# A 64x64 triangular solve in a delta-rule recurrence: blocks of 16 and doubling, or blocks of 32 and substitution

## The chip, the core and the metric

The kernel runs on one core of a Trainium2 chip. The core has five instruction streams that run beside each other and wait for one another through semaphores: the tensor engine (PE, with its weight loads as PEld), VectorE (DVE), ScalarE (ACT), GpSimd (POOL) and SyncE (SP), which here only issues DMAs. Each stream runs its instructions strictly in the order in which they stand. The metric is the device time of one execution in microseconds, as the median of the runs; lower is better.

## What is computed

The reference is a two-layer decoder trunk over 512 tokens of width 1024. Each layer projects its input once and feeds four branches: a delta-rule recurrence (RWKV-7, 8 heads of 64), latent attention, a convolution module and cross-attention. Each branch is gated and projected, the four are merged with sigmoid gates, projected again and normalised. The part that matters here is the recurrence:

```python
def step(state, inp):
    r_t, w_t, k_t, v_t, a_t, b_t = inp
    sa = jnp.einsum('bhvk,bhk->bhv', state, a_t)
    state = (state * w_t[:, :, None, :] + sa[..., None] * b_t[:, :, None, :]
             + v_t[..., None] * k_t[:, :, None, :])
    return state, jnp.einsum('bhvk,bhk->bhv', state, r_t)

s0 = jnp.zeros((B, H, N, N), jnp.float32)
_, y = lax.scan(step, s0, xs)
```

Token by token this would be 512 dependent steps. The kernel takes 64 tokens at a time: inside such a chunk the terms `sa` depend on each other through a strictly triangular 64x64 matrix, so a triangular system has to be solved for each head and chunk; the rest is matrix products.

## The kernel before

**Order.** The kernel is Python that records instructions. A planner (class `Plan`) keeps a clock for each engine and prices each instruction as it is recorded: an instruction on GpSimd, say, at 250 ns and 1.6 ns for each element of a partition, with 105 ns more where it needs the one before it. There is one main stream of tensor work, the items (projections, attention, merges), and beside it many tasks, written as generators. When the planned PE clock reaches the time at which a task can go on, the task's next piece is recorded; otherwise the main stream's next piece is, usually three to fifteen wide matmuls. `plan.due(x)` puts off a task until x is there by the planner's reckoning, and a `yield` of a condition until a counter allows it. A piece that takes PSUM space with "small" is gathered with others, up to 3000 ns, so that PE changes less often between 128x128 tiles and 64x64 ones. What results is one fixed order for each engine and for the SP queue; at run time nothing is reordered, and an engine whose next operand is late waits.

**Units.** The recurrence of a layer is cut into eight units, each of one pair of heads (`j`) and half the tokens (`hf`), so four chunks of two heads, which are eight triangular systems of 64. `rwkv_unit` is the task of one. Several units run overlapped, held apart by counters: `subs` (substitutions done), `mids`, `toks`, `chains`, `units`. The steps of a unit, by the names of their tiles:

- `zw`, `th`, `cum`, `D`, `E`, `bt`, `kt`, `AR`: decay, keys and queries of the unit.
- `g`: the products that give the triangular matrices; VectorE scales and masks them into `M`. A unit could take `g` only when all units before it had finished their substitution (`L["subs"] == un`).
- `Mc`: the diagonal 16x16 blocks of M (four in each system, 32 in a unit), gathered by the block mask `bm`.
- `substitution()`: Mc goes by DMA to a scratch in DRAM (`d1`) and comes back as `W`, one block on each of 32 partitions. GpSimd makes a copy with ones on the diagonal (`zz`, half of `ZT`) and inverts the blocks by 14 steps of two instructions each, then makes a transposed copy. Both go to DRAM (`d2`) and come back as `zc` and `tc`.
- VectorE spreads them into block-diagonal `Z` and `T`. Two rounds of doubling follow on PE: `x0` and `x1` (products with M), `dt`, `dz` and `dy` (products with the inverse so far), each result copied or merged by a mask (`lvm`) on ScalarE or VectorE. After them Z holds the whole inverse of each 64x64 system.
- `nv` (tile `x`, from `NQ` and `vt`) gives half of the right side `RA`; `va` multiplies the inverse by RA.
- `gb`, `hh`, `y0`, `w0` to `w3`, `yb`, `ty`: the chunk's transfer matrices, the chain of states, the outputs and their transposition.

Where other work is: the gate projections `xg`, `mg`, `cg`, `rg`, the merges (`ps_m` and `po`) of branches 3, 1, 2 and 0 in this order, of which the last needs the recurrence's end, and the convolution's taps (`cacc`, on VectorE), its normalisation (`conv_norm`, with the transposes `ct` and `cb`) run in the same time. Weights come in blocks of 512 KB, some blocks ahead of their use, through the same SP queue as the substitution's DMAs.

The tensor engine's products of 64x64 tiles use one quarter of the array each; with `four=True` the planner prices them as running in four quarters at once.

Of the kernel before, what the change touches and what calls it, by code (L numbers as in the profile page):

```python
# [46 lines left out]
for _n, _c in _PARTS:  # L47
# [6 lines left out]
    ("minc", 64), ("bm", 4), ("id2", 64),  # L54
# [207 lines left out]
def trunk_kernel(ctx: ExitStack, tc: tile.TileContext, A, out, dbg=None):  # L262
# [76 lines left out]
    lvm = cp.tile([128, 3, 64], U8, tag="lvm", name="lvm")  # L339
# [3 lines left out]
    scr = [[dp.tile([32 * (n + 1), 256], F32, tag=f"scr{n}{i}", name=f"scr{n}{i}").rearrange("a b -> (a b)") for n in range(2)] for i in range(2)]  # L343
# [13 lines left out]
    def constants():  # L357
        DMA(cst, A["cst"])
        t = u("lvm32", 192, I32)
        DMA(t, A["lvm"])  # L360
        once = u("once", 272)
        DMA(once, A["once"])
        pi = cp.tile([128, 4], I32, tag="pos", name="pos")
        DMA(pi, A["pos"])

        def run():
            V.tensor_copy(lvm, t.rearrange("p (a b) -> p a b", a=3))
# [216 lines left out]
    def layer_items(l):  # L584
# [62 lines left out]
        def begin_rwkv(get):  # L647
# [6 lines left out]
            L["blk"] = [L["rp"].tile([32] + n, F32, tag=x, name=x + t_) for x, n in (("W", [16, 16]), ("ZT", [2, 16, 16]), ("tmpW", [56]))]  # L654
            L["X"] = L["rp"].tile([128, 4, 64], F32, tag="X", name="X" + t_)
            G.memset(L["X"], 0.0)
# [34 lines left out]
        L["units"] = L["chains"] = L["toks"] = L["mids"] = L["subs"] = L["next"] = L["read"] = 0  # L691
# [9 lines left out]
        def rwkv_unit(j, hf, r, k, v):  # L701
# [50 lines left out]
            yield lambda: L["subs"] == un  # L752
# [23 lines left out]
            W, ZT, tmp = L["blk"]  # L776

            zt = []

            def substitution():  # L780
# [8 lines left out]
                plan.due(W)  # L789
                yield  # L790
                zz = ZT[:, 0]
                G.tensor_scalar(out=zz, in0=W, scalar1=1.0, scalar2=0.0, op0=ALU.mult, op1=ALU.add)
                G.memset(zz.rearrange("p a b -> p (a b)")[:, 0:256:17], 1.0)
# [12 lines left out]
                plan.due(d2)  # L806
                yield
                zc, tc_ = rk2("zc", "zc" + t, [4, 16], 2), rk2("tc", "tc" + t, [4, 16], 2)
                dz, dt = (d2[4 * 128 * 16 * i:4 * 128 * 16 * (i + 1)] for i in range(2))
                DMA(tc_, dt.rearrange("(e p t) -> p e t", e=4, t=16))  # L810
                dz = dz.rearrange("(h c p t) -> h p c t", h=2, c=4, t=16)
                for h in range(2):
                    DMA(zc[HALF[h]], dz[h])
                zt.extend((zc, tc_))
                L["subs"] += 1
# [58 lines left out]

            yield lambda: L["subs"] > un
            zc, tc_ = zt
            plan.due(zc, tc_)
            yield
            Z, T, X = rk2("Z", "Z" + t, [4, 64]), rk2("T", "T" + t, [4, 64]), L["X"]
            for dst, src in ((T, tc_), (Z[:, 0:2], chunks(zc)[:, 0]), (Z[:, 2:4], chunks(zc)[:, 1])):  # L880
                n = src.shape[1]
                V.tensor_tensor(out=dst.rearrange("p c (b t) -> p c b t", b=4), in0=src.unsqueeze(2).to_broadcast([128, n, 4, 16]),
                                in1=bm.unsqueeze(1).unsqueeze(3).to_broadcast([128, n, 4, 16]), op=ALU.mult)
            yield

            def second(x, i):

                return x.rearrange("p e (d i k) -> p e d i k", d=2, i=2)[:, :, :, i, :]

            def pairs(x, i):  # L890
                return x.rearrange("p e w -> p (e w)").rearrange("p (e q i k) -> p e q i k", e=2, q=4, i=2)[:, :, :, i, :]

            def four(x):
                return x.rearrange("p e a (d k) -> p e (a d) k", d=2)

            x0, = yield from pg.take([128, 2, 512], "x0" + t, 1, "small")
            xv, nv = (x.rearrange("p c (a w) -> p c a w", a=2) for x in (x0[:, :, 0:64], x0[:, :, 64:192]))
            for cp, c2, h in quads:
                MM(xv[HALF[h], c2, cp].rearrange("p (d k) -> p d k", d=2), M[HALF[c2], 2 * h + cp], second(T, 0)[HALF[c2], 2 * h + cp], start=True, stop=True, four=True)
# [3 lines left out]
            S.copy(pairs(X, 0), four(xv))  # L903
            V.tensor_copy(by2(RA)[:, :, :, 0:64], nv)
            pg.free()
            yield
            x0, = yield from pg.take([128, 2, 512], "dt" + t)
            dT = x0[:, :, 0:64].rearrange("p c (a w) -> p c a w", a=2)
            dz, = yield from pa.take([128, 2, 2, 32], "dz" + t, 1, "small")
            for cp, c2, h in quads:  # L910
                e = 2 * c2 + cp
                MM(dT[HALF[c2], h, cp].rearrange("p (d k) -> p d k", d=2), Z[HALF[h], e], second(X, 0)[HALF[h], e], start=True, stop=True, four=True)
            for cp, c2, h in quads:
                e = 2 * c2 + cp
                MM(dz[HALF[h], c2, cp].rearrange("p (d k) -> p d k", d=2), X[HALF[h], e], second(Z, 1)[HALF[h], e], start=True, stop=True)
            yield

            def lv(i):
                return lvm[:, i, :].rearrange("p (q k) -> p q k", q=4).unsqueeze(1).to_broadcast([128, 2, 4, 16])

            V.copy_predicated(pairs(T, 0), lv(0), four(dT))
# [916 lines left out]
def _constants():  # L1838
    c = {}
# [91 lines left out]
```

## Time and profile before

| what | before |
|---|---|
| median of 3 runs | 1556.57 us (1556.33 to 1556.65) |
| the profiled execution | 1563.89 us |
| its span, first to last instruction | 1562.1 us |
| mean granted clock of PE | 0.994 |
| DMA | 153.34 MB in 81366 packets, 98 GB/s mean |
| recurrence, layer 1: first `g` to last `ty` | 268.5 to about 632 us |
| recurrence, layer 2: the same | 1080.0 to about 1413 us |

The profile is of one execution, which is 7.3 us longer than the median of the runs. Times are microseconds from the start of the span. In a row of instructions the columns are the start, the duration, the engine, the line, the operation and `output<-inputs` with sizes as partitions x elements; numbers of buffers are left out, so tiles of the same name in different units stand under one name. A matmul of 32-bit numbers in these tiles has two records, so eight matmuls show as 16. In a row of windows stand the stretch, its length, the busy time with the number of instructions, the granted clock, the share of DMA and its rate. Lines point to helpers that record every instruction (L231 for VectorE, ScalarE and GpSimd, L282 and L287 for PE, L294 for DMAs), so the tile's name tells more than the line.

### The profile page before, as it was taken

How to read it: one execution, taken by the hardware profiler on the slowest of the kernel's cores; microseconds unless marked ns; L12 is line 12 of the kernel's file. 1: busy time of each engine (PE TensorE's matmuls, PEld its weight loads, DVE VectorE, ACT ScalarE, POOL GpSimd, SP SyncE). 2: the span in 40 equal slices, each digit the busy share in tenths (PEclk: the TensorE clock that was granted, in tenths of full speed). 3: DMA queues.
4: the chain of work that ended last, by engine and by line, in shares of the span. 5: the costliest groups of instructions: out<-in, count | busy, mean ns of one | idle time of the engine just before them, and what ended most of it. 6: DMA issues, size and time to landing. Idle time of an engine off the chain costs nothing.

```text
span 1562.1 us, 32041 instructions
## 1 busy us (share of the span) xinstructions
PE 1536.9 (98%) x12848; PEld 1278.8 (82%) x12848; DVE 1110.7 (71%) x2460; ACT 643.2 (41%) x1387; POOL 238.9 (15%) x588
## 2 busy tenths in 40 slices
PE   8999999999999999999999999999999999999997
PEld 8987788778787887888998877788787887778887
DVE  5789888888665764545555878888987667645567
ACT  5546654433333332334364454534433333323332
POOL 0000000533214330000000000001633333300002
PEclk9999999999999999999999999999999999999999
DMA  6452422222222132423343243332222222225222
GB/s 209 133 153 63 115 82 82 91 85 60 86 83 75 62 89 82 148 95 114 119 153 107 82 107 94 93 103 84 75 72 76 74 73 91 74 86 194 89 91 82
DMA packets 81366, 153.34 MB, mean 98 GB/s; under 512 B 33216, under 2 KB 39360, under 8 KB 81216
## 3 DMA queue, kind: packets, MB, share of 16 engines
q1 hardware_dynamic: 81216, 151.28, 31.3%
q8 instruction: 101, 1.65, 0.4%
q14 instruction: 49, 0.40, 0.1%
HBM read 133.95 MB, written 5.77 MB: 89 GB/s over the span
## 4 chain that ended last, share of the span: by engine, by line
PE 91%; DVE 4%; DMA 2%; ACT 1%; issue 1%; POOL 0%; SPq 0%; ACTq 0%; DVEq 0%; POOLq 0%
PE ps_m L282 23%; PE po L282 11%; PE pz L282 3%; PE ps_cg L282 3%; PE ps_xg L282 3%; PE ps_r L282 3%; PE ps_v L282 3%; PE ps_k L282 3%; PE ps_val L282 3%; PE ps_rg L282 3%; PE ps_xq L282 3%; PE ps_mg L282 3%; PE ps_glu L282 2%; PE ms L282 2%; PE pl L282 2%; PE mo L282 1%
## 5 line engine op out<-in xcount | busy, mean ns | idle before, releaser
L231 DVE SCALAR_TENSOR_TENSOR cacc<-hpad,prm,cacc 128x512 f32<-128x512 f32 x240 | 180.2, 753 | 3.4
L231 ACT ACTIVATE tm<-ps_m,prm 128x512 f32<-128x512 f32 x64 | 44.1, 689 | 135.1 <-PE ps_m L282 135.1
L231 DVE SCALAR_TENSOR_TENSOR mt<-tm,po 128x512 f32<-128x512 f32 x48 | 33.0, 688 | 89.7 <-PE po L282 85.0
L231 POOL TENSOR_TENSOR tmpW<-ZT,W 32x14 f32<-32x14 f32 (+6 forms) x224 | 86.6, 387 | 15.9
L231 POOL TENSOR_TENSOR ZT<-ZT,tmpW 32x14 f32<-32x14 f32 (+6 forms) x224 | 85.4, 381 | 17.5
L231 POOL MEMSET X<- 128x256 f32 x2 | 0.6, 314 | 326.1 <-DVE mo L231 167.6
L231 POOL TENSOR_SCALAR gr<-gm 128x4 f32<-128x4 f32 x16 | 3.7, 233 | 292.2 <-DVE gm L231 292.2
L231 POOL TENSOR_SCALAR lrs<-lmv 128x1 f32<-128x1 f32 x8 | 2.2, 273 | 295.7 <-DVE lmv L231 295.7
L231 POOL TENSOR_SCALAR ZT<-W 32x256 f32<-32x256 f32 x16 | 7.9, 491 | 233.1 <-DMA W<-scr 233.1
L231 ACT ACTIVATE mP<-ms,nmm 128x128 f32<-128x128 f32 (+3 forms) x64 | 33.6, 527 | 20.3 <-DVE nmm L231 17.5
L231 DVE TENSOR_TENSOR merged<-merged,mt 128x512 f32<-128x512 f32 x48 | 33.3, 694 | 1.7
L231 DVE SCALAR_TENSOR_TENSOR S<-w,dpad,H 128x64 f32<-128x64 f32 x48 | 13.5, 281 | 28.3 <-PE w L282 28.3
L231 DVE TENSOR_REDUCE nmm<-ms 128x1 f32<-128x128 f32 (+3 forms) x64 | 30.4, 485 | 1.9 <-PE ms L282 1.4
L231 ACT COPY mPT<-mt 128x128 f32<-128x128 f32 (+3 forms) x64 | 26.1, 429 | 10.4 <-PE mt L287 10.0
L287 PE MATMUL mt<-cst,mP 128*128 128x128 f32 x160 | 27.3, 280 | 0.5 <-DVE smm L231 0.2
L231 DVE TENSOR_SCALAR mP<-mP,smm 128x128 f32<-128x128 f32 (+3 forms) x64 | 24.8, 387 | 2.3
L231 ACT CAST rbh<-w 128x256 fp32r<-128x256 f32 x16 | 6.5, 407 | 48.2 <-DVE w L231 48.2
L282 PE MATMUL mo<-mPT,v 128*64 128x128 f32 x320 | 24.6, 284 | 0.0
L287 PEld LDWEIGHTS mt<-cst,mP 128*128 128x128 f32 x160 | 19.0, 142 | 6.2 <-issue 1.2
L231 ACT ACTIVATE xP<-xs,nmx 128x256 f32<-128x256 f32 x32 | 15.2, 476 | 20.1 <-DVE nmx L231 19.9
L282 PE MATMUL ms<-kTl,qT 96*128 96x128 f32 (+3 forms) x64 | 23.3, 363 | 0.0
L231 ACT COPY X<-x 128x128 f32<-128x128 f32 x32 | 8.4, 264 | 35.3 <-PE x L282 35.2
(3357 smaller groups left out, 5603.7 us busy)
## 6 DMA issues: line engine op xcount, KB each, us to landing
w<-in_w_ch_dram SPq DMA_DIRECT2D x146, 512.0 KB, 3.5
w<-in_w_o_dram SPq DMA_DIRECT2D x32, 512.0 KB, 3.4
w<-in_w_out_dram SPq DMA_DIRECT2D x16, 512.0 KB, 3.5
w<-in_w_lat_dram SPq DMA_DIRECT2D x16, 336.0 KB, 3.1
w<-in_w_mk_dram SPq DMA_DIRECT2D x8, 512.0 KB, 3.4
w<-in_w_mv_dram SPq DMA_DIRECT2D x8, 512.0 KB, 3.8
w<-in_w_qk_dram SPq DMA_DIRECT2D x8, 320.0 KB, 2.9
x<-in_xT_dram SPq DMA_DIRECT2D x8, 256.0 KB, 5.8
```

The lines of the kernel that those rows point to most:

```text
L231: return self.plan.keep(f(*a, **k))
L282: plan.keep(nc.tensor.matmul(o, lhsT, rhs, start=start, stop=stop))
L287: plan.keep(nc.tensor.transpose(o, i, ident))
```

## The change

The diagonal blocks are now 32x32, two in each system, 16 in a unit. `W` holds each of them on eight partitions (one DMA reads the 64 KB scratch eight times over, 512 KB in all), and each of the eight partitions solves four of the 32 rows of the inverse: `zz` starts as rows of the identity matrix (`idz`, loaded by DMA for each unit), and 31 steps of two GpSimd instructions on 128 partitions solve them, with one to four rows in each instruction as the rows become active. Only one copy of the result goes to DRAM; four DMAs bring it back into the two diagonal blocks of `Z`, a tile that lives through the layer and whose other blocks are zero. The whole 64x64 inverse is no longer formed. Instead the right side is substituted: `s1` multiplies Z by RA, `Y1` keeps the first 32 tokens of it, `s2` multiplies M by Y1, the second 32 tokens of that are added to RA, and `va` multiplies Z by this RA. `nv` has a tile of its own (`n0`) and runs before the wait for the solve. The tiles `T`, `X`, `ZT`, `zc`, `tc` and the masks `lvm` go.

The waits change too: `g` may be taken when the substitutions of all units but the one before are done and that far the systems are solved (`subs >= un - 1` and `solved >= un - 1`); loads into Z wait until the unit before has made its `va`. In the convolution's normalisation, the second transposes (`cb`) wait until four merges of branch 1 are done.

```diff
-            yield lambda: L["subs"] == un
+            yield lambda: L["subs"] >= un - 1 and L["solved"] >= un - 1
...
-            Mc = rk2("Mc", "Mc" + t, [4, 16])
-            V.tensor_scalar(out=Mc, in0=M[:, :, 0:16], scalar1=bm[:, 0:1], scalar2=None, op0=ALU.mult)
-            for b in range(1, 4):
-                V.scalar_tensor_tensor(out=Mc, in0=M[:, :, 16 * b:16 * b + 16], scalar=bm[:, b:b + 1], in1=Mc, op0=ALU.mult, op1=ALU.add)
+            Mc = rk2("Mc", "Mc" + t, [4, 32])
+            V.tensor_scalar(out=Mc, in0=M[:, :, 0:32], scalar1=bm[:, 0:1], scalar2=None, op0=ALU.mult)
+            V.scalar_tensor_tensor(out=Mc, in0=M[:, :, 32:64], scalar=bm[:, 1:2], in1=Mc, op0=ALU.mult, op1=ALU.add)
...
-                DMA(d1.rearrange("(c p t) -> p c t", c=4, t=16), Mc)
+                DMA(d1.rearrange("(c p t) -> p c t", c=4, t=32), Mc)
+                yield lambda: L["subs"] == un
+                DMA(zz, A["idz"].rearrange("p (a b) -> p a b", a=4), "zz" + t)
                 plan.due(d1)
                 yield
-                DMA(W.rearrange("p a b -> p (a b)"), d1.rearrange("(q e) -> q e", q=32), "W" + t)
+                DMA(W.rearrange("p a b -> p (a b)"), d1.rearrange("(q e) -> q e", q=16).unsqueeze(0).to_broadcast([8, 16, 1024]), "W" + t)
...
-                for q in range(1, 15):
-                    n = 15 - q
-                    o = tmp[:, 0:q * n].rearrange("p (a b) -> p a b", a=q)
-                    G.tensor_tensor(out=o, in0=zz[:, 0:q, q:q + 1].to_broadcast([32, q, n]),
-                                    in1=W[:, q:q + 1, q + 1:16].to_broadcast([32, q, n]), op=ALU.mult)
-                    G.tensor_tensor(out=zz[:, 0:q, q + 1:16], in0=zz[:, 0:q, q + 1:16], in1=o, op=ALU.add)
+                for q in range(31):
+                    m, n = q // 8 + 1, 31 - q
+                    o = tmp[:, 0:m * n].rearrange("p (a b) -> p a b", a=m)
+                    G.tensor_tensor(out=o, in0=zz[:, 0:m, q:q + 1].to_broadcast([128, m, n]),
+                                    in1=W[:, q:q + 1, q + 1:32].to_broadcast([128, m, n]), op=ALU.mult)
+                    G.tensor_tensor(out=zz[:, 0:m, q + 1:32], in0=zz[:, 0:m, q + 1:32], in1=o, op=ALU.add)
                     if q % 2:
                         yield
-                G.tensor_scalar(out=ZT[:, 1], in0=zz.rearrange("p a b -> p b a"), scalar1=1.0, scalar2=0.0, op0=ALU.mult, op1=ALU.add)
-                plan.due(ZT)
-                yield
-                DMA(d2.rearrange("(z q e) -> q z e", z=2, q=32), ZT.rearrange("p z a b -> p z (a b)"))
+                plan.due(zz)
+                yield
+                DMA(d2.rearrange("(a p t) -> p a t", a=4, t=32), zz)
+                L["subs"] += 1
                 plan.due(d2)
-                yield
...
+                yield lambda: L["solved"] == un
+                dz = d2.rearrange("(i h e b t) -> h b i e t", i=32, h=2, e=4, b=2)
                 for h in range(2):
-                    DMA(zc[HALF[h]], dz[h])
...
+                    for b in range(2):
+                        DMA(Z[64 * h + 32 * b:64 * h + 32 * b + 32, :, 32 * b:32 * b + 32], dz[h, b], f"Z{h}{b}" + t)
+                plan.done[Z.tensor.name] = plan.done["Z11" + t]
+                L["solve"] += 1
...
+            yield lambda: L["solve"] > un
+            plan.due(Z, RA)
+            yield
+            y1, = yield from pg.take([128, 2, 512], "s1" + t, 1, "small")
+            yv = y1[:, :, 0:256].rearrange("p h (a w) -> p h a w", a=2)
             for cp, c2, h in quads:
...
+                MM(yv[HALF[c2], h, cp], Z[HALF[h], 2 * cp + c2], RA[HALF[h], 2 * c2 + cp], start=True, stop=True, four=True)
+            yield
+            Y1 = rk2("Y1", "Y1" + t, [4, 128])
+            S.activation(by2(Y1), yv, AF.Copy, scale=bm[:, 0:1])
+            pg.free()
+            yield
+            r2, = yield from pg.take([128, 2, 512], "s2" + t, 1, "small")
+            rv = r2[:, :, 0:256].rearrange("p c (a w) -> p c a w", a=2)
             for cp, c2, h in quads:
...
+                MM(rv[HALF[h], c2, cp], M[HALF[c2], 2 * h + cp], Y1[HALF[c2], 2 * h + cp], start=True, stop=True, four=True)
+            yield
+            V.scalar_tensor_tensor(out=by2(RA), in0=rv, scalar=bm[:, 1:2], in1=by2(RA), op0=ALU.mult, op1=ALU.add)
             pg.free()
...
+            L["solved"] += 1
...
                 ntok.append(n)
                 yield
+            yield lambda: added[1] >= 4
             for i in range(4):
                 ps, = yield from pa.take([128, 512], f"cb{i}" + t_)
```

More of the change, by code (lines that the diff above doesn't have):

```diff
@@ L690, in layer_items @@
         L["yr"] = [None] * 4
-        L["units"] = L["chains"] = L["toks"] = L["mids"] = L["subs"] = L["next"] = L["read"] = 0
+        L["units"] = L["chains"] = L["toks"] = L["mids"] = L["subs"] = L["solve"] = L["solved"] = L["next"] = L["read"] = 0
         L["front"] = False
@@ L872, in rwkv_unit @@
             L["toks"] += 1
-            yield lambda: L["subs"] > un
-            zc, tc_ = zt
-            plan.due(zc, tc_)
-            yield
[L879 to L899, printed above, removed]
+            n0, = yield from pg.take([128, 2, 512], "n0" + t, 1, "small")
+            nv = n0[:, :, 0:128].rearrange("p c (a w) -> p c a w", a=2)
             for cp, c2, h in quads:
@@ L916, in rwkv_unit @@
-            yield
-            def lv(i):
-                return lvm[:, i, :].rearrange("p (q k) -> p q k", q=4).unsqueeze(1).to_broadcast([128, 2, 4, 16])
-            V.copy_predicated(pairs(T, 0), lv(0), four(dT))
-            V.copy_predicated(pairs(Z, 1), lv(1), four(dz))
-            pg.free()
-            pa.free()
-            yield
-            x1, = yield from pg.take([128, 2, 512], "x1" + t, 1, "small")
-            xv = x1[:, :, 0:64].rearrange("p c (a w) -> p c a w", a=2)
-            for cp, c2, h in quads:
-                MM(xv[HALF[h], c2, cp], M[HALF[c2], 2 * h + cp], T[HALF[c2], 2 * h + cp, 0:32], start=True, stop=True, four=True)
```

60 lines of the change are left out of this document (14 added, 46 removed).

## The prediction

> **What bounds the kernel now.** I read the page first, then the chain of waits, then the tensor engine's timeline in the middle of the recurrence.
>
> ```profile
> span 1562.1 us, 32041 instructions
> PE 1536.9 (98%) x12848; PEld 1278.8 (82%) x12848; DVE 1110.7 (71%) x2460; ACT 643.2 (41%) x1387; POOL 238.9 (15%) x588
> PE 91%; DVE 4%; DMA 2%; ACT 1%; issue 1%; POOL 0%; SPq 0%; ACTq 0%; DVEq 0%; POOLq 0%
> ```
>
> PE is busy for 1536.9 of 1562.1 us and makes 91% of the chain. The other work, projections and merges, fills PE while the recurrence's short steps wait. So two things count: the PE time of the recurrence's own products, and whether PE, which runs its instructions in a fixed order, reaches a product before its operand is there. GpSimd (POOL) has 15%: it is no bound as a sum, but each solve is a series of dependent instructions.
>
> The recurrence's products are 64x64 tiles that interrupt the stream of 128x128 ones. Five such detours of one unit, each with the last wide matmul before it, its first group and the third wide matmul after it (start, duration):
>
> ```profile
> 485.23 0.39 PE L282 MATMUL ps_m<-xh,w73l 128*128 128x512 f32 x1
> 485.55 0.43 PE L282 MATMUL x<-T,M 64*64 64x32 f32 x16
> ...
> 486.74 0.40 PE L282 MATMUL ps_m<-xh,w73l 128*128 128x512 f32 x1
> ...
> 490.33 0.28 PE L282 MATMUL zw<-lxa,lla 128*128 128x256 f32 x1
> 490.54 0.43 PE L282 MATMUL dt<-X,Z 64*64 64x32 f32 x16
> ...
> 491.94 0.40 PE L282 MATMUL ps_m<-xh,w75l 128*128 128x512 f32 x1
> ...
> 494.70 0.39 PE L282 MATMUL ps_m<-xh,w75l 128*128 128x512 f32 x1
> 495.01 0.43 PE L282 MATMUL x<-T,M 64*64 64x32 f32 x16
> ...
> 495.95 0.40 PE L282 MATMUL ps_m<-xh,w75l 128*128 128x512 f32 x1
> ...
> 498.69 0.39 PE L282 MATMUL po<-ymg1h,w74l 128*128 128x512 f32 x1
> 499.01 0.66 PE L282 MATMUL dy<-Z,X 64*64 64x32 f32 x16
> ...
> 500.16 0.40 PE L282 MATMUL po<-ymg2h,w74l 128*128 128x512 f32 x1
> ...
> 502.90 0.39 PE L282 MATMUL ps_m<-xh,w76l 128*128 128x512 f32 x1
> 503.22 0.67 PE L282 MATMUL va<-RA,Z 64*64 64x128 f32 x16
> ...
> 504.39 0.39 PE L282 MATMUL ps_m<-xh,w76l 128*128 128x512 f32 x1
> ```
>
> Between 495.95 and 498.69 lie 12 steps of the wide stream, 0.228 us each. Three such steps would take 0.68 us; what a stretch takes beyond that is the detour's price: x with the NQ product 1.51 - 0.68 = 0.83 us, dt with dz 1.61 - 0.57 = 1.04 (the step from 490.33 has half the columns), the second x 1.25 - 0.68 = 0.57, dy 1.47 - 0.68 = 0.79, va 1.49 - 0.68 = 0.81. The NQ product adds 0.26 to an x that costs 0.57 alone, so about 0.31 of a detour is the price of leaving and returning.
>
> **Tensor work.** There are 16 units (two layers of eight). The change removes the x products with T (two groups), dt, dz and dy: 0.83 + 1.04 + 0.57 + 0.79 = 3.23 us a unit, with NQ among it. It leaves NQ as a detour (about 0.57, as the second x) and adds s1 and s2, each of va's shape (0.81 each): 2.19 us. Difference 1.04 x 16 = 16.6 us. In the built order, detours fall from 139 to 129 and not by the 16 that this assumes, because the old groups more often shared one: 6 x 0.31 = 1.9 us back. The tensor term is **-14.8 us** (9904 matmuls become 9520). Bounds: -14.8 less another 4 if the new groups share detours better, and -11 if s1 and s2 run as dy does for its width; I take the middle because va is the very same shape.
>
> **The solve on GpSimd.** Before, 28 dependent TENSOR_TENSOR on 32 partitions and three preparing steps; now 62 on 128 partitions, none preparing, with 30 elements per partition on average where there were 41.
>
> ```profile
> 276.12 0.40 POOL L231 TENSOR_SCALAR ZT<-W 32x256 f32<-32x256 f32 x1 [71.22 <-DMA W<-scr]
> 276.65 0.20 POOL L231 TENSOR_TENSOR tmpW<-ZT,W 32x14 f32<-32x14 f32 x1
> 276.93 0.20 POOL L231 TENSOR_TENSOR ZT<-ZT,tmpW 32x14 f32<-32x14 f32 x1
> ```
>
> ```profile
> L231 POOL TENSOR_TENSOR z<-z,ln_b x4: 729/738/785, 1539.0 to 1556.7; 128x256 f32<-128x256 f32 x4
> ```
>
> Then busy time of these instructions alone (tile tmpW) in four stretches, one unit's solve in each, and of VectorE in two of them:
>
> ```profile
> 276.00:290.00 14.00, 11.04 (x28) 1.00 0.31 112
> 302.00:318.00 16.00, 12.30 (x28) 1.00 0.30 99
> 489.00:502.00 13.00, 9.31 (x28) 1.00 0.26 83
> 1088.00:1104.00 16.00, 13.31 (x28) 1.00 0.20 77
> ```
>
> ```profile
> 489.00:502.00 13.00, 7.73 (x16) 1.00 0.26 83
> 1088.00:1104.00 16.00, 15.43 (x27) 1.00 0.20 77
> ```
>
> A free instruction on 14 elements takes 0.20 us, with 0.08 to the next. On 128 partitions and 256 elements it takes 0.738: (0.738 - 0.20) / 242 = 0.0022 us an element, so four times the partitions are taken as free, and 11 elements fewer save 0.02. The mean is 0.33 us where VectorE is busy for 7.73 of 13 us, and 0.475 where it is busy for 15.43 of 16 us. A solve now takes 62 x (mean - 0.02 + 0.08): **28.1 us** at the first stretch's pace (0.394), 30.9 at the second's (0.439), 24.4 in quiet ones (0.333), 33.2 at the worst (0.475). Bound below: 62 x (0.20 + 0.035 + 0.08) = 19.5 us, never hindered.
>
> [...] The two pairs of rows agree: slow solves stand where VectorE is full. [...]
>
> **When the solve must be done.** The first unit's path from g to the solved block (engine, queue and issue rows), with two landings and the queue's wait:
>
> ```profile
> 268.51 0.46 PE L282 MATMUL g<-AR,bt 64*64 64x64 f32 x16
> ```
>
> ```profile
> 271.96 0.39 SPq L294 DMA_DIRECT2D scr<-Mc  x1
> 273.82 0.34 SPq L294 DMA_DIRECT2D W<-scr  x1
> ...
> 290.57 0.34 SPq L294 DMA_DIRECT2D scr<-ZT  x1
> 292.21 0.38 SPq L294 DMA_DIRECT2D tc<-scr  x1
> 292.63 1.31 SPq L294 DMA_DIRECT2D zc<-scr  x2
> ```
>
> ```profile
> w<-in_w_ch_dram SPq DMA_DIRECT2D x146, 512.0 KB, 3.5
> ...
> W<-scr SPq DMA_DIRECT2D x16, 32.0 KB, 1.7
> zc<-scr SPq DMA_DIRECT2D x32, 16.0 KB, 2.2
> ```
>
> ```profile
> SPq L294 <- POOL ZT L231: 155.7, 16, 14.9
> ```
>
> Now, outside the solve: g to the issue of Mc 3.45, less about 0.45 for two Mc steps fewer = 3.0; landing and the issue of W 1.86; W to GpSimd 2.3, but W is 512 KB instead of 32, priced as a weight load: 2.3 - 1.7 + 3.5 = 4.1; writing the result 1.64; the next unit's zz and W issues, about 0.75, in front; four Z loads issued at 0.65 each, the last 1.95 after the first; landing 2.2. Sum 15.5 us. W's source is read eight times over; no row shows that, so 3.5 stands between 1.7 (its bytes in the scratch did not grow eightfold) and 7 (twice a weight load).
>
> In the changed order, PE has between the first unit's g and its s1 159 matmuls of 512 columns, 12 of 256 and four detours: 159 x 0.227 + 12 x 0.12 + 4.3 = 41.7 us. Need 15.5 + 28.1 = 43.6: late by 1.9. The second unit's solve can start only when the first has left W: 6.5 us (1.64 + 0.75 + 4.1) after its end, and its s1 stands 33.3 us of tensor work behind the first one's: 30.9 + 6.5 - 33.3 = 4.1 late. In layer 2 the same two have 41.7 and 33.6: 15.5 + 33.2 - 41.7 = 7.0 and 30.9 + 6.5 - 33.6 = 3.8. In quiet units 15.5 + 24.4 = 39.9 stays under 41 and 24.4 + 6.5 = 30.9 under 31.7, the shortest spacing in the order: nothing. Together 16.8 us late. Since what PE waits for stops VectorE too, the end of a late solve runs at the quiet pace; bounds 0 and 16.8, and I take half, **+8.4 us**.
>
> **What I cost at nothing.** s1, the masked copy Y1 on ScalarE, s2, the addition to RA on VectorE and va follow each other with 15 wide matmuls (3.4 us) between; one pass over 128x512 and its hand-over fit, and without that cover each unit would pay about 1 us twice. VectorE loses more work than it gains, and is not on the path. SP issues eight DMAs a unit for six, at about 0.4 to 0.65 us; its write of the solve stands in front of weight loads, and so does zz, which waits for that write. Before, SP waited there for 155.7 us in 16 times and PE's waits showed none of it, since weights are held ahead; if that cover went, each late solve would cost its lateness again. Holding back the convolution's last transposes until four merges of the latent-attention branch (the condition on added[1]) moves the same instructions; it takes VectorE work from the fourth unit's solve to the fifth's, which has 47 us from g to s1.
>
> **The sum.** 1563.89 (the profiled execution; span 1562.1) - 14.8 + 8.4 = 1557.5. The median of the runs is 1556.57, 7.3 below the profiled time, so **1550** for the median. This kernel's measurement tells 0.2%, about 3 us, from no change.
>
> **Rivals.**
> - All hidden: solves end in time, and only the tensor term counts: 1556.6 - 14.8 = 1542. For it: quiet units have room. Against: the order leaves the first units 41.7 us. Chance 17%.
> - Cancelled: the four units pay in full: -14.8 + 16.8 = +2, 1558.6. For it: their windows were full of VectorE work before. Against: that work stops when PE does. Chance 15%.
> - Slower, the solve paces the recurrence: one buffer for W and zz makes solves follow each other, and at 0.439 (30.9 us) eleven units are late by 4.4 us on average, 48 us; half of it, as above, gives 24 - 14.8 = +9, 1566, and all of it 1590. It decides from 0.93 us a unit (14.8 / 16). For it: the spacings of 32 to 33 us. Against: the later units' solves ran at 0.33. Chance 25%. [...]
> - It doesn't do what it says: the broadcast load of W takes 7 us instead of 3.5; eleven close units pay 3.5 each, 38 us, half of it 19: 1550 + 19 = 1569. Chance 5%.
> - The forecast, 1545 to 1554: 38%.
>
> Faster takes the first, and nearly all of the forecast: 53%. Same, 16%; slower, 31%. The likeliest case alone spans 1545 to 1554; the range reaches 1538 (the tensor term's better bound, nothing late) and 1570, past the slower cases' nearer ends.
>
> **What would show it.** Right: s1 and s2 detours at 0.81 us; 62 solve instructions at 0.31 to 0.45 us; PE waits at s1 in the first two units of each layer, none in the later ones; windows between the recurrence's phases unchanged. Wrong: PE waiting at s1 in most units, W landing later than 4 us, or PE waiting for weights behind SP.

## The result and the profile after

The changed kernel takes **1627.38 us** (median of 4 runs, 1622.51 to 1628.41) against 1556.55 us for the kernel before, measured beside it (4 runs, 1556.33 to 1556.65). The ratio is **1.0435**, 95% interval 1.042 to 1.0451. The forecast was 1550, the range ended at 1570: the sign was wrong, and the time lies 57 us beyond the range.

Four lines of the page of the changed kernel: span, busy times, the chain of waits by engine, and the group of the solve's multiplications.

```profile
span 1626.3 us, 30915 instructions
...
PE 1541.3 (95%) x12080; PEld 1271.4 (78%) x12080; DVE 1091.1 (67%) x2347; ACT 645.8 (40%) x1371; POOL 365.4 (22%) x1084
...
PE 67%; DMA 11%; POOL 9%; DVE 7%; issue 3%; ACT 2%; SPq 1%; ACTq 0%; POOLq 0%; DVEq 0%
...
L231 POOL TENSOR_TENSOR tmpW<-zz,W 128x24 f32<-128x24 f32 (+23 forms) x496 | 159.8, 322 | 359.7 <-DMA W<-scr 322.9
```

Span less PE's busy time is what PE stood still: 85.0 us, where it was 1562.1 - 1536.9 = 25.2. PE's share of the chain fell from 91% to 67%; most of the missing part went to transfers (2% to 11%) and GpSimd (0% to 9%). The last line hints at which transfer: of the 359.7 us for which GpSimd stood idle before its multiplications, 322.9 ended with the landing of W. It is a hint only, since most of this is the time between two units' solves. In the kernel before, GpSimd's first step on each W waited for it too:

```profile
L231 POOL TENSOR_SCALAR ZT<-W 32x256 f32<-32x256 f32 x16 | 7.9, 491 | 233.1 <-DMA W<-scr 233.1
```

Where PE waited at the recurrence's products (operation, what it waited for; total, times, longest, all in us):

```profile
PE s L282 <- DMA Z<-scr: 18.9, 7, 7.4
PE s L282 <- POOL tmpW L231: 11.3, 1, 11.3
PE ty L287 <- DVE yb L231: 6.3, 3, 4.2
...
PE va L282 <- DVE RA L231: 5.2, 3, 2.8
PE n L282 <- DVE NQ L231: 4.2, 2, 2.4
```

The same for SP's queue:

```profile
SPq L294 <- POOL zz L231: 175.1, 16, 22.1
SPq L294 <- DMA w<-in_w_ch_dram: 121.1, 40, 9.2
```

The second of these in the kernel before:

```profile
SPq L294 <- DMA w<-in_w_ch_dram: 50.2, 31, 3.8
```

In the kernel before, PE's waits at the recurrence's products were next to nothing (the longest at a product of a unit is 0.5 us). Now the s products wait for 31.6 us, counting one wait of 1.4 us for VectorE. A further 28 us of new idle time stand elsewhere: mostly at `ty`, `va`, `n` and `w` of the recurrence, and at products whose weights are late. That they follow from a late s or from late weights is argued here; experiment 1 comes back to it.

Idle time is 59.8 us of the loss. The rest is PE at half speed. First the span of the kernel before with its mean granted clock:

```profile
core 0: 1562.1 us, clock 0.994
```

The same of the changed kernel:

```profile
core 0: 1626.3 us, clock 0.983
```

And three windows of the changed kernel, during a wait for Z and after it (the columns are length, PE busy, weight loads, VectorE, ScalarE, GpSimd, granted clock, DMA share, GB/s):

```profile
315.37:319.46 4.09, 0.00 (x0) 0.03 (x1) 1.35 (x2) 0.00 (x0) 0.45 (x2) 0.99 1.04 208
319.46:322.82 3.36, 3.36 (x21) 2.62 (x22) 1.94 (x3) 2.33 (x4) 2.73 (x9) 0.50 0.22 84
322.82:326.18 3.36, 3.36 (x29) 2.46 (x28) 1.70 (x4) 0.62 (x1) 2.73 (x9) 1.00 0.47 143
```

A wait of 4.09 us is followed by 3.36 us at a granted clock of 0.50, and then full speed again. In the traces of these two kernels the clock is 1.00 or 0.50 and nothing between, so the time at half speed is estimated as twice the shortfall of the mean: 2 x 0.017 x 1626.3, about 55 us, against about 19 before (the traces' clock records add up to 54.2 and 17.5). That is 36 us more, of which half, 18, is lost.

So the spans add up: -14.8 (the tensor term as forecast) + 59.8 (idle) + 18 (half speed) = +63, where 1626.3 - 1562.1 = 64.2.

**One unit, step by step.** Rows of the changed kernel's timeline for the first unit of layer 2 (start, duration, engine or queue, operation, idle before and its end):

```profile
1106.16 0.46 PE L282 MATMUL g<-AR,bt 64*64 64x64 f32 x16
...
1110.95 0.64 SPq L294 DMA_DIRECT2D W<-scr  x1
1111.69 0.40 SPq L294 DMA_DIRECT2D w<-in_w_ch_dram  x1
...
1119.22 0.24 POOL L231 TENSOR_TENSOR tmpW<-zz,W 128x31 f32<-128x31 f32 x1 [107.31 <-DMA W<-scr]
...
1149.39 0.71 POOL L231 TENSOR_TENSOR zz<-zz,tmpW 128x4 f32<-128x4 f32 x1
...
1150.13 0.38 SPq L294 DMA_DIRECT2D scr<-zz  x1
1151.96 0.33 SPq L294 DMA_DIRECT2D zz<-in_idz_dram  x1
1152.34 0.63 SPq L294 DMA_DIRECT2D W<-scr  x1
1153.07 0.40 SPq L294 DMA_DIRECT2D w<-in_w_o_dram  x1
1153.52 1.85 SPq L294 DMA_DIRECT2D Z<-scr  x4
...
1161.92 1.51 PE L282 MATMUL s<-RA,Z 64*64 64x128 f32 x16 [11.29 <-POOL tmpW L231]
```

| step | forecast, us | measured, us |
|---|---|---|
| g to the issue of W | 3.0 + 1.86 = 4.86 | 4.79 |
| issue of W to GpSimd's first instruction | 4.1 | **8.27** |
| the solve | 33.2 (its worst) | 30.88 |
| end of the solve to the first Z issue | 1.64 + 0.75 = 2.39 | 3.42 |
| first Z issue to s | 1.95 + 2.2 = 4.15 | **8.40** |
| sum | 48.7 | 55.76 |

The arithmetic on GpSimd came in under its forecast. Two landings account for the excess: W takes twice what it was given, and the four Z loads take 4.25 us more, while the next unit's 512 KB W and a weight load, issued up to 1.2 us before them, are still moving (experiment 3 tests that they are the cause). PE had 44.5 us of other work and small waits between g and the stop at s, so 11.29 of the 55.76 us were left to wait for. The releaser in the last row is misleading: GpSimd had been done for 11.8 us, and it was the Z loads that came last.

**Why W is slow.** A window in which W moves nearly alone (it was issued at 398.51; the last packets of the weight load issued before it land at the start of the window):

```profile
401.00:404.20 3.20, 3.20 (x31) 2.37 (x29) 2.80 (x9) 2.37 (x5) 0.00 (x0) 1.00 0.52 138
```

The DMA engines are busy to 0.52 of all sixteen, at 138 GB/s, and for most of the window the trace shows eight 4 KB packets under way at once. W's source names its eight copies as the outermost size: `unsqueeze(0).to_broadcast([8, 16, 1024])`. Eight of sixteen engines would be 0.50, near the 0.52 measured; that it is the place of the copies that keeps the load to half of them, the window alone doesn't show. Whether the eightfold reading of the same 64 KB is slow by itself is the rival that the first experiment decides.

### The profile page after: what moved, and what is told of

It reads as the page before. It is cut to its first block, busy times and chain, and to the rows that moved or that the text cites. A ratio compares the mean times of both kernels' runs of the same rounds, so it can differ in the third digit from the quotient of the medians.

```text
span 1626.3 us, 30915 instructions
## 1 busy us (share of the span) xinstructions
PE 1541.3 (95%) x12080; PEld 1271.4 (78%) x12080; DVE 1091.1 (67%) x2347; ACT 645.8 (40%) x1371; POOL 365.4 (22%) x1084
## 4 chain that ended last, share of the span: by engine, by line
PE 67%; DMA 11%; POOL 9%; DVE 7%; issue 3%; ACT 2%; SPq 1%; ACTq 0%; POOLq 0%; DVEq 0%
PE ps_m L282 16%; PE po L282 8%; POOL tmpW L231 4%; POOL zz L231 4%; DMA W<-scr 4%; PE pz L282 3%; PE ps_val L282 3%; PE ps_rg L282 3%; PE ps_xq L282 3%; PE ps_xg L282 2%; PE ps_glu L282 2%; PE ms L282 2%; DMA w<-in_w_ch_dram 2%; PE pl L282 2%; PE ps_r L282 2%
## 5 line engine op out<-in xcount | busy, mean ns | idle before, releaser
L231 POOL TENSOR_TENSOR tmpW<-zz,W 128x24 f32<-128x24 f32 (+23 forms) x496 | 159.8, 322 | 359.7 <-DMA W<-scr 322.9
L231 POOL TENSOR_TENSOR zz<-zz,tmpW 128x24 f32<-128x24 f32 (+23 forms) x496 | 160.1, 323 | 38.8
L282 PE MATMUL s<-RA,Z 64*64 64x128 f32 x256 | 15.2, 318 | 31.6 <-DMA Z<-scr 18.9
L282 PEld LDWEIGHTS s<-RA,Z 64*64 64x64 f32 x256 | 9.9, 152 | 37.9 <-issue 14.2
L231 DVE SCALAR_TENSOR_TENSOR S<-w,dpad,H 128x64 f32<-128x64 f32 x48 | 13.4, 280 | 29.6 <-PE w L282 29.4
L231 ACT ACTIVATE Y<-s,cst 128x512 f32<-128x512 f32 x16 | 11.0, 687 | 37.9 <-PE s L282 37.8
L231 ACT COPY Y<-y 128x256 f32<-128x256 f32 x16 | 6.0, 372 | 46.1 <-PE y L282 46.1
```

The source lines that it names most:

```text
L231: return self.plan.keep(f(*a, **k))
L282: plan.keep(nc.tensor.matmul(o, lhsT, rhs, start=start, stop=stop))
```

## The experiments

Theory A: the loads of W and Z land later than the order of instructions allows for, W because it uses half of the engines, Z because W stands ahead of it; PE waits, and each longer wait brings half speed. Rival B: the repeated read is what is slow. Rival C: GpSimd's pace, with one buffer for W and zz, sets the recurrence. Rival D: SP, waiting for a solve's result, holds weights back. Rival E: the held-back transposes. In the table, idle is span less PE busy, and "at s" the sum of PE's waits at s products. The last four columns are of the profiled execution, which in some kernels lay 4 to 5 us from the median (W in halves: 1567.12), so these columns can't rank kernels whose medians lie within a few us.

| kernel | median, us | ratio to before (95%) | span | PE busy | idle | at s |
|---|---|---|---|---|---|---|
| changed | 1627.38 | 1.0435 (1.042 to 1.0451) | 1626.3 | 1541.3 | 85.0 | 31.6 |
| W on all engines | 1595.42 | 1.0228 (1.0203 to 1.0252) | 1597.3 | 1537.5 | 59.8 | 24.4 |
| later prices | 1603.82 | 1.0284 (1.0263 to 1.0305) | 1602.3 | 1538.7 | 63.6 | 15.3 |
| Z loads first | 1600.81 | 1.0261 (1.0235 to 1.0287) | 1594.2 | 1533.7 | 60.5 | 8.5 |
| transposes not held back | 1633.85 | 1.047 (1.0451 to 1.0489) | 1633.2 | 1544.0 | 89.2 | 44.6 |
| W on all engines, counted prices | 1582.02 | 1.0142 (1.0122 to 1.0162) | 1576.6 | 1528.9 | 47.7 | 13.0 |
| the same, Z loads first | 1576.70 | 1.0106 (1.0078 to 1.0134) | 1577.2 | 1530.6 | 46.6 | 4.3 |
| the same without it, 3 us of slack | 1568.34 | 1.0057 (1.0039 to 1.0075) | 1567.5 | 1525.4 | 42.1 | 1.6 |
| two buffers | 1567.98 | 1.0052 (1.0035 to 1.0069) | 1568.1 | 1526.2 | 41.9 | 1.2 |
| W in halves | 1561.76 | 1.0012 (1.0 to 1.0023) | 1565.0 | 1527.6 | 37.4 | 5.1 |
| W in halves, more slack | 1568.39 | 1.006 (1.0042 to 1.0077) | 1565.7 | 1525.3 | 40.4 | 1.2 |
| W in halves, two long solves | **1553.15** | **0.9958 (0.9946 to 0.997)** | 1553.7 | 1523.5 | 30.2 | 1.2 |
| the same, a little more slack | 1557.33 | 0.9993 (0.998 to 1.0005) | 1555.6 | 1521.0 | 34.6 | 2.0 |

**1. W on all engines.** Only W's load, the numbering of the partitions and the write of the result differ; the order on PE, VectorE, ScalarE and GpSimd is the changed kernel's.

```
- d1.rearrange("(q e) -> q e", q=16).unsqueeze(0).to_broadcast([8, 16, 1024])
+ d1.rearrange("(q e) -> q e", q=16).unsqueeze(1).to_broadcast([16, 8, 1024])
- DMA(d2.rearrange("(a p t) -> p a t", a=4, t=32), zz)
+ plan.dma(512 * 128, _names(d2), _names(zz))
+ dw = d2.rearrange("(a g q t) -> a q g t", a=4, g=8, t=32)
+ for a in range(4):
+     plan.keep(nc.sync.dma_start(dw[a], zz[:, a]))
- idz = np.repeat(....reshape(8, 128), 16, 0)
+ idz = np.tile(....reshape(8, 128), (16, 1))
```

> What it does: the partitions of W and zz are numbered with the block first and the row group second, so that the source of W's load has 16 as its outermost size and the eight-fold repetition inside it; the result of a solve is then written in four pieces of 16 KB instead of one of 64 KB. The order of the tensor engine's, VectorE's, ScalarE's and GpSimd's instructions is that of the changed kernel; SP has three issues more a unit. Theory A (W's load uses only half of the transfer engines, since its outermost size is 8: the trace shows eight packets at once while W moves alone): from W's issue to GpSimd's first instruction 4 to 6 us where it was 8.2; the last Z load lands about 1 to 3 us sooner where W runs ahead of it, less 1.5 us for the three issues more; PE's gaps fall from 73 us by 15 to 35 us, and with the half-speed stretches behind them the time falls from 1627 to 1575 to 1605. Rival B (reading the same 64 KB eight times is slow as such): W's issue to GpSimd stays above 7 us and the time is 1627 to 1640. Rival C (GpSimd's own pace makes the solves late, and the load of W matters little): W's load is shorter but the time stays above 1615.

A window of this kernel in which W moves alone:

```profile
274.30:274.90 0.60, 0.60 (x4) 0.49 (x3) 0.00 (x0) 0.14 (x1) 0.00 (x0) 1.00 0.92 294
```

And the two ends of that load in its timeline:

```profile
272.87 0.58 SPq L294 DMA_DIRECT2D W<-scr  x1
...
277.99 0.53 POOL L231 TENSOR_TENSOR tmpW<-zz,W 128x31 f32<-128x31 f32 x1 [102.29 <-DMA W<-scr]
```

The same eightfold read now fills the engines (0.92 of sixteen, 294 GB/s), and GpSimd starts 5.1 us after the issue, with weight loads right behind W. Rival B is out. The time falls by 32 us in an unchanged order, as theory A expected, in spite of three more issues a unit on SP. Waits at s fall only from 31.6 to 24.4. Of the 25.2 us of idle time that go, 18 stood elsewhere; since PE's order is the same, these too came from W's lateness.

**2. Later prices.** The planner is told that W and Z come later, so that s stands later on PE.

```
- plan.done[W.tensor.name] = plan.done["W" + t]
+ plan.done[W.tensor.name] = (plan.done["W" + t][0] + 4500.0, "DMA")
- plan.done[Z.tensor.name] = plan.done["Z11" + t]
+ plan.done[Z.tensor.name] = (plan.done["Z11" + t][0] + 3000.0, "DMA")
```

> What it does: the planner that sets the order of the instructions is told that W is there 4.5 us later, and Z 3 us later, than it worked out before; nothing else changes. The first s product then stands about 5 to 9 us of tensor work later behind g. Theory A (the loads of W and Z arrive later than the order allows for, and PE waits for what the order promised): the waits at s go from 31 us to under 8, the half-speed stretches with them, and the time falls to 1555 to 1590; what is left of the 60 us of new gaps stands at other places. Rival C (the solves follow each other on one buffer at their own pace): the later s pushes the next solve back too, waits stay, and the time stays above 1600. Rival D (SP, waiting for GpSimd's result, holds back the weights): waits at s go, those at the weights' users stay or grow, and the time is 1590 to 1620.

1603.82 us, 24 us less, but 14 us above theory A's range, and inside the ranges of rivals C and D. Waits at s fall to 15.3 us, not under 8. PE's longest waits at the recurrence's products in this kernel:

```profile
PE s L282 <- DMA Z<-scr: 12.8, 7, 4.5
PE ty L287 <- DVE yb L231: 7.0, 2, 3.5
...
PE n L282 <- DVE NQ L231: 5.5, 2, 3.5
PE zw L282 <- DVE yc L231: 4.2, 1, 4.2
```

The waits at s halve, where rival C had them stay, and others grow: each layer's recurrence now ends with a wait of 3.5 us at its last `ty`, which suggests that with s placed later less wide work is left to cover its end. Rival D's sign, weights' users that wait as long or longer, is not there: the two waits at `ps_rg` for a weight fall from 1.7 us each to 0.3. No theory gets both its time and its waits right here.

**3. Z loads first.**

```
- yield lambda: L["subs"] == un
+ yield lambda: L["subs"] == un and L["solve"] == un
  DMA(zz, A["idz"]..., "zz" + t)
```

> What it does: the identity and W of a unit are loaded only when the four Z loads of the unit before have been issued; before, they went ahead of them where the order allowed it. Theory A (W's 512 KB in front of the Z loads is part of the lateness): last Z issue to s falls from 6.5 to about 2.5 us in the units where W went ahead, the next solve starts 2 to 3 us later; the time falls by 10 to 30 us. Rival C (pace of the chained solves): the delay of the next solve costs as much as the earlier Z saves, within 10 us of 1627.

1600.81 us, 27 us less. In the unit shown above, SP's rows are now:

```profile
1137.55 0.38 SPq L294 DMA_DIRECT2D scr<-zz  x1
1138.03 0.45 SPq L294 DMA_DIRECT2D w<-in_w_o_dram  x1
1139.37 1.75 SPq L294 DMA_DIRECT2D Z<-scr  x4
1141.16 0.43 SPq L294 DMA_DIRECT2D zz<-in_idz_dram  x1
1141.64 0.62 SPq L294 DMA_DIRECT2D W<-scr  x1
```

Its s starts at 1142.2: 2.8 us after the first Z issue, where it took 8.40. A weight load still goes out 1.3 us ahead of the Z loads, so W's place is the main thing that differs: W ahead of Z is shown as the second part of the lateness. The next solve starts 12.9 us after this one's end, where it took 10.3; this delay of 2.6 us cost less than the earlier Z gained, against rival C.

**4. Transposes not held back.**

```
- yield lambda: added[1] >= 4
```

> What it does: takes out the condition that holds the convolution's last four transposes back until four merges of the latent-attention branch; the solve is as in the changed kernel. Theory A (the loss comes from late loads of W and Z): the time stays within 15 us of 1627, since the order is shuffled but the loads are the same. Rival E (holding the transposes back starves the middle of the layers): the time falls by more than 20 us.

1633.85 us, 6 us slower: rival E is out.

**5 to 8. Repairs together.** All four have W on all engines and a planner that counts the four writes as four issues. The first adds 1.2 us to W and 1.5 us to Z, as read from the trace of experiment 1; the second adds 3 us to each; the third is the first with the Z loads ahead; the fourth is the first with two buffers for W and zz, paid for with one of six pairs of weight buffers.

```
- L["blk"] = [... (("W", [32, 32]), ("zz", [4, 32]), ("tmpW", [48]))]
+ L["blk"] = [... (("W0", [32, 32]), ("zz0", [4, 32]), ("W1", [32, 32]), ("zz1", [4, 32]), ("tmpW", [48]))]
- yield lambda: L["subs"] == un
+ yield lambda: L["subs"] >= un - 1
  DMA(zz, ...)
...
+ yield lambda: L["subs"] == un
  for q in range(31):
```

> What it does: the new numbering of W's partitions (W's load on all transfer engines), together with a planner that counts what the trace of that kernel shows: W 1.2 us later than it worked out, the four writes of the result as four issues, Z 1.5 us later. Theory A (late loads against an order that promised them earlier): the two repairs add up, waits at s fall from 24 us to under 10, the time is 1550 to 1580. Rival C (the chain of solves on one buffer paces the recurrence): the later s pushes the next g back, waits stay, 1585 to 1605.

> What it does: as the kernel with the new numbering and the counted prices, but W counted 3 us late and Z 3 us late, so with about 3 us of slack at each solve. Theory A: waits at s nearly gone (under 4 us), time 1545 to 1575, unless the later order lacks wide tensor work at the end of the recurrence, which would show as waits at the last units' w and ty. Rival C: no better than the kernel with exact prices, by more than 5 us slower.

> What it does: new numbering, counted prices, and the Z loads of a unit ahead of the next unit's identity and W. Theory A: all three repairs attack the same lateness, so they don't add up: 1550 to 1580, within 12 us of the kernel without the third. Rival C: putting W behind the Z loads delays the next solve by 2 to 3 us, so 10 us or more slower than without it.

> What it does: new numbering, counted prices, and two buffers each for W and zz, so that a unit's W is loaded while the unit before is being solved; for the 4.5 KB per partition one pair of the six pairs of split weight buffers is given up. Theory A (late loads): the load of W leaves the chain between two solves; GpSimd starts a chained solve within 1 us of the last one's end; waits at s under 6 us; 1545 to 1575, if five weight buffers suffice. Rival C in its strong form (one buffer paces the recurrence) expects the largest gain of all here: 10 us or more below the kernel with one buffer. Rival F (weights one buffer short): waits at ps_m and po for weights, time above 1585.

1582.02, 1568.34, 1576.70 and 1567.98 us. The first missed theory A's range by 2 us, and its waits at s fell to 13.0 us, not under 10; rival C's range began at 1585. Putting the Z loads first brought 5 us, where rival C expected a loss of 10 or more. With 3 us of slack the waits at s are gone (1.6 us) and the time falls by another 14 us, where rival C expected more than 5 us of loss. The two buffers bring 14 us as well; the strong form of C had expected that too, so this run shows only that W's load in the chain between two solves costs time, not that the solves do. It also rules out rival F, which needed more than 1585. What remains in the kernel with slack:

```profile
PE ty L287 <- DVE yb L231: 7.0, 2, 3.6
...
PE w L282 <- DVE S L231: 1.9, 2, 1.5
PE s L282 <- DMA Z<-scr: 1.6, 1, 1.6
```

The ty waits stand at the end of each layer's recurrence (642.67 and about 1421); the kernel before has none there. With slack in every unit the recurrence outlasts the wide work that covers it. In this mild form rival C is right.

**9 and 10. W in halves.** The load is taken out of the chain without more memory: two tiles of 16 pivots, the changed kernel's numbering (with which W's load kept 0.52 of the engines busy) and one write of the result. `L["half"]` is raised when the solve before has used its pivot 15.

```
+ wv = [d1.rearrange("(q h e) -> h q e", q=16, h=2)[h].unsqueeze(0).to_broadcast([8, 16, 512]) for h in range(2)]
- yield lambda: L["subs"] == un
+ yield lambda: L["half"] == un
  DMA(zz, ...)
- DMA(W..., "W" + t)
+ DMA(Wa.rearrange("p a b -> p (a b)"), wv[0], "Wa" + t)
...
+ yield lambda: L["subs"] == un
  for q in range(31):
+     if q == 7:
+         DMA(Wb.rearrange("p a b -> p (a b)"), wv[1], "Wb" + t)
```

> What it does: the changed kernel with its own numbering of the partitions (W's load on half of the transfer engines), but W in two tiles of 16 pivots each, 256 KB a load. The first half is loaded as soon as the solve before has used its own first half, the second during the solve, after the former unit's Z loads; the identity has two buffers. The planner counts each half 1.2 us and Z 0.5 us later than it worked out. Theory A (late loads): GpSimd goes from one chained solve to the next within 1 us, no W stands ahead of Z loads, waits at s under 6 us, and the time is 1545 to 1572. Rival C in its strong form: solves chain without a gap here, so the spacing of s falls to the solve's 26 to 30 us and 10 us or more are won over the best kernel so far (1568). Rival G (SP waits for the first half of a solve and holds back weights): waits at ps_m or po for weights, time above 1580.

> What it does: as the kernel with W in halves, but each half is counted 2.5 us and Z 2 us late. Theory A: if the first already has no waits at s, more slack brings nothing there and makes the recurrence end later: waits at the last units' w and ty; 1550 to 1575, within 8 us of the first. If the first still waits at s by more than 10 us, this one is the faster by that.

1561.76 us, level with the kernel before, and 1568.39 with more slack, both in theory A's ranges; the strong form of C had expected 10 us under 1568, and rival G more than 1580. The largest wait left in the first of them among the recurrence's products, on PE, with what SP and ScalarE did before it:

```profile
338.63 0.38 SPq L294 DMA_DIRECT2D scr<-zz  x1
339.11 1.67 SPq L294 DMA_DIRECT2D w<-in_w_ch_dram  x1
...
343.81 1.14 ACT L231 CAST w55h<-w 128x512 fp32r<-128x512 f32 x2 [9.80 <-DMA w<-in_w_ch_dram]
...
346.67 0.37 PE L282 MATMUL yb<-zero,B 64*64 64x64 f32 x2 [4.48 <-DVE M L231]
```

The second unit's result is written when its solve ends, and the weight load behind it in SP's queue goes out right after. ScalarE had been waiting for that weight for 9.80 us, VectorE stood behind it, and PE behind VectorE. That is rival D, at one place: a solve longer than planned blocks SP's queue.

The kernel with more slack has the same chain at the same unit, and it is longer there:

```profile
PE ct L287 <- DVE cn L231: 7.8, 1, 7.8
```

Its second unit's result is written at 339.68, the weight load goes out at 340.16, and ScalarE waits 9.08 us for that weight, VectorE 7.45 us for ScalarE and PE 7.79 us for VectorE. The waits that theory A named, at the layers' last `ty`, are there, with 2.1 us each. Against the first of the two kernels, the waits at `ty` grow by 4.9 us and the one behind the blocked queue by 3.3, while those at s shrink by 3.9.

**11 and 12. Two long solves counted as such.**

```
  G.tensor_tensor(out=zz[:, 0:m, q + 1:32], ...)
+ if un < 2:
+     plan.op("POOL", 60.0, _names(zz), [])
```

> What it does: the kernel with W in halves (1561.8 us, one wait of 4.5 us where the weights stood on SP behind the second unit's result), and the planner told that the solves of the first two units of a layer take 5 us longer than it worked out, as the traces show for them (29 to 31 us against 25). The write of their result is then placed later in SP's order, behind weight loads, and their s later on PE. Theory A with D (late result holds back SP, and weights come late): the wait at yb and the waits at s in the first two units go, with the half-speed stretches behind them, 8 to 15 us: 1546 to 1556, a little below the kernel before. Rival C: the later s of two units makes the chain of each layer longer by 3 to 5 us, which shows as waits at the last units, and the time stays within 1558 to 1568.

> What it does: as the other of this call, with 1.5 us instead of 1.2 us more for each half of W, 1 us instead of 0.5 us more for Z, and 5.7 us instead of 5 us more for the first two solves (W is still read in halves through half of the transfer engines, the label notwithstanding). Theory A: within 6 us of the other; if the other still waits at s by more than 5 us, this is the faster. Rival C: slower than the other by 3 us or more, with the waits at the last units' w and ty.

**1553.15 us**, ratio 0.9958 (0.9946 to 0.997): faster than the changed kernel, and 0.4% faster than the kernel before. The unit of the table again, in this kernel's timeline:

```profile
1076.50 0.46 PE L282 MATMUL g<-AR,bt 64*64 64x64 f32 x16
...
1081.31 0.64 SPq L294 DMA_DIRECT2D Wa<-scr  x1
...
1086.02 0.24 POOL L231 TENSOR_TENSOR tmpW<-zz,Wa 128x31 f32<-128x31 f32 x1 [103.77 <-DMA Wa<-scr]
...
1117.30 0.38 SPq L294 DMA_DIRECT2D scr<-zz  x1
1119.12 1.75 SPq L294 DMA_DIRECT2D Z<-scr  x4
...
1123.93 0.67 PE L282 MATMUL s<-RA,Z 64*64 64x128 f32 x16
```

And the busy times of its page:

```profile
PE 1523.5 (98%) x12080; PEld 1262.7 (81%) x12080; DVE 1092.0 (70%) x2347; ACT 646.5 (42%) x1371; POOL 387.5 (25%) x1084
```

The solve takes as long as before (31.2 us); 4.7 us after the issue it has its half of W, 1.8 us after the write the Z loads go out, and s doesn't wait. With GpSimd doing the same 62 instructions at the same pace, the loss of 71 us has become a gain of 6. The last kernel, with a little more slack, was 4 us slower. That is within theory A's 6 us, and rival C's "3 us or more" fits as well; but its waits at the layers' last `w` and `ty`, C's sign, are absent.

## Why the prediction was wrong

- **Tensor work: right.** -14.8 us was forecast. In the changed kernel PE's busy time rose by 4.4 us, but 18 of that is half speed, so the work itself fell by about 13.6. In the best kernel, with about as much half speed as the kernel before, it is 1523.5 us against 1536.9: -13.4.
- **The solve on GpSimd: right.** In the changed kernel 62 instructions took 22.1 to 31.5 us, with a mean near 26, against 24.4 to 33.2. GpSimd was not slowed by 128 partitions (its first instruction in the unit shown, on 128x31, took 0.24 us), nor the bound. Two slips in the sums change nothing: the steps before had 40 elements on average, not 41, and 159 x 0.227 + 12 x 0.12 + 4.3 is 41.8, not 41.7.
- **The failed step: W "priced as a weight load".** The value was 4.1 us from issue to GpSimd; it measured 8.27 in the unit shown, and 7.2 to 10.0 in all sixteen. The load kept 0.52 of the sixteen engines busy, against 0.92 with the copies inside. The bound "7 (twice a weight load)" named the size nearly, but for a repeated read, and the rival that used it priced one load alone: it gave 1569.
- **The second failed step: the Z landing of 2.2 us.** It was taken from transfers with nothing large ahead of them. The prediction itself placed the next unit's W "in front" of the Z loads and charged 0.75 us for its issue, none for its 512 KB. Over the whole kernel the median landing stayed near the forecast, at 2.4 us, but the longest took 7.5.
- **"Half of the lateness."** The discount assumed that a late solve ends at the quiet pace once PE has stopped. In the unit shown PE stopped when the solve was over: the late part was transfers, which the pace of GpSimd doesn't touch, and 11.29 us were paid where 7.0 was the full forecast. The units were not the forecast ones either: PE waited at the first s of units 1, 5 and 7 in layer 1 and 1, 3, 5 and 7 in layer 2, and at no second unit, where 4.1 and 3.8 us were forecast.
- **SP's cover, "at nothing".** Its waits that end with a weight load went from 50.2 to 121.1 us. "If that cover went, each late solve would cost its lateness again" is about what the 28 us outside s amount to. Experiments 9 and 10 show such a chain, at one unit each. For the changed kernel it is argued from the fact that 18 of the 28 go when W is faster in the same order.
- **Half speed after a wait** was in no term: 18 us.
- **"The solve paces the recurrence"** ended on the right side by the wrong mechanism. What followed the solves was their transfers; with these repaired the same solves fit.

Between the best kernel's -6 us and the tensor term of -14.8 lie 8.8 us. Idle time takes 5.0 of them (30.2 against 25.2), and the tensor term was 1.4 too large. The other 2.4 are no work at all: the profiled execution of the kernel before, on which the sum was made, took 4.8 us more than the median measured beside this kernel (1563.89 against 1559.14), that of this kernel 2.3 more (1555.47 against 1553.15).

## What to carry to other kernels

Price a transfer by its access pattern, not by its bytes: with the broadcast as the outermost size the load kept 0.52 of the engines busy here, with it inside 0.92, and that alone was worth 32 us of 1627. Where an order is fixed ahead, charge small loads on the critical path for every large one issued just before them (in the unit shown, s came 8.40 us after the first Z issue with W ahead and 2.8 with W behind), and give a long wait in a shared queue the price of all that stands behind it (9.80 us on ScalarE for one weight in experiment 9). Slack is best placed where a wait shows that it is missing: from the kernel with W in halves, at 1562, counting two of eight solves as long gave 1553, and more slack in every unit 1568, with the queue still blocked at the same place and new waits at the recurrence's ends.

## What the hardware showed beside this

A wait on PE can cost more than itself: the one of 4.09 us above had 3.36 us at a clock of 0.50 behind it. Over the fourteen profiled executions of this study, leaving out the first 60 us of each, all 22 waits above 4 us were followed by a stretch of half speed, 26 of 38 between 2 and 4 us, and 29 of 109 between 1 and 2 us. The stretches came in multiples of 3.41 us, but for the one that runs past each kernel's end.

Within an execution all these stretches start whole multiples of 3.413 us apart, so an execution can be divided into windows of that length and counted window by window. While the clock was whole, none of 5961 windows in which PE stood still for less than 1.37 us was followed by half speed, and all 66 with 1.8 us or more were; of the 61 between, 21 were. In these traces, then, the drop went by how much of a wait fell into one window: a wait of 2 us could go free where it straddled two, as the one of 2.25 us at 1294.27 in the changed kernel did, and none went free that lay in a single window.

The engine that a profile names as the end of a wait can be wrong by far: the wait of 11.29 us put down to GpSimd ended with a DMA that had been issued 3.4 us after GpSimd was done.
